# RWKV prep in a two-layer decoder trunk: weight splits of the k, r and v projections issued ahead, both pieces of a tile together

## The chip, the core and the metric

The kernel runs as one launch on one NeuronCore of a Trainium2 chip. The metric is the device time of one execution in microseconds (us); lower is better. Engines are named as in the profile: PE (TensorE matmul), DVE (VectorE), ACT (ScalarE), POOL (GpSimd), SP (SyncE, which here issues nearly all DMAs), and PEld for PE's weight loads.

## What is computed

Two layers, each on 512 tokens of width 1024 in float32. Of one layer:

```
h   = RMSNorm(x)
[q,k,v | r,k,v,lora_w,lora_a,lora_g | gate_A,gate_B] = h @ W_in
A   = sliding-window attention(q,k,v) -> W_oA
B   = RWKV-7 time mixing(r,k,v,decay,iclr,g) -> W_oB
x  += RMSNorm((sigmoid(gate_A)*A + sigmoid(gate_B)*B) @ W_out)
x  += RMSNorm(W_down(gelu(a)*b)),  [a,b] = causal conv3(RMSNorm(x) @ W_up)
x  += RMSNorm(sigmoid(x @ W_pg) * (p[i] @ W_ple))
```

The time mixing is a recurrence per head (16 heads of 64):

```
def step(state, inp):
    r_t, w_t, k_t, v_t, a_t, b_t = inp
    sa = einsum('bhvk,bhk->bhv', state, a_t)
    state = state * w_t[:,:,None,:] + sa[...,None] * b_t[:,:,None,:] + v_t[...,None] * k_t[:,:,None,:]
    return state, einsum('bhvk,bhk->bhv', state, r_t)
```

## The kernel before

Activations lie transposed, 128 channels by 512 tokens to a tile, eight tiles for h. Float32 products are made of three passes in a reduced type: weight and activation are each split into a high and a low part, and `mm3` (lines 247 to 252) issues high x high (L250), high x low (L251) and low x high (L252) into the same PSUM tile. A projection of one output tile has 8 such triples, 24 matmuls, and its weights come in two pieces of four row blocks (128 x 512 elements, 256 KB each). `load_w` (line 136) handles a piece in three steps: SP issues the DMA into `w`, ACT copies it into `wh` (L125), and DVE writes `wl = w - wh` (L155). Of the class "m" there are 2 buffers for `w`, 3 for `wh` and 3 for `wl` (line 141). `proj` (line 254) loads one piece, issues its 12 matmuls, loads the next piece, issues its 12; `whole` (line 208) loads both pieces before any matmul. Two PSUM tiles `pm` and one `pf` take the results.

The RWKV part of a layer works in four groups of two preps (`rwkv_group`, line 738). A prep (`rwkv_prep`, line 585) handles one channel tile, two heads: projection k, two small lora matmuls (`thw`, `tha`), a decay scan on DVE, the tile `AR`, projection r, small masked products `A` (PSUM, 2 buffers, written out by DVE as `AM`), transposes `bkT`, projection v, and transposes of v. In the text the preps of a layer are counted from 0 to 7, so prep 5 is the second of group 2 when groups are counted from 0 to 3. After two preps `rwkv_inverse` (line 672) inverts a triangular system: 31 steps of two short DVE operations each (L697, L699), a round trip through DRAM (`zd` out, eight DMAs `Z` back), and then, per prep of the group, a chain PE, ACT, PE, ACT/DVE of 32 x 32 products (t1 at L718, z12 at L727). Then eight scan steps over chunks of 64 tokens follow (L770 to L797), each a chain PE, DVE/ACT, PE, DVE/ACT, PE, DVE, and a group norm on DVE whose result is transposed on PE (`yt`, L822) and stored.

Beside this stand the gate projection (`w_gb`, matmuls on `pf` and `pm`) and, after it, the output projection of attention (`att_out`, `w_oa`, 8 tiles), whose 512-column matmuls can be put between the small ones; then the projection `w_or` reads what the four groups stored (`yr`).

No order is written out by hand. A scheduler orders each engine's instructions when the program is built: by its own estimates of times it takes the next instruction that could run, preferring the one that stands earlier in the program. `high_priority(offset=n)` lets the instructions of a block count as if they stood n places earlier. At run time each engine, SP's DMA queue included, works strictly in the order that was built.

Of the kernel before, what the change touches and what calls it, by code (L numbers as in the profile page):

```python
# [19 lines left out]
P = 128  # L20
T = 512
DM = 1024
KT = DM // P
# [32 lines left out]
class Trunk:  # L56
# [528 lines left out]
    def rwkv_prep(self, l, j, gi, R, X2, DC, ssp, nd):  # L585
        nc, a, h, vv, dv, rp = self.nc, self.a, self.h, self.vv, self.dv, R.rp
        NP_ = 32
        c1 = slice(j, j + 1)
        Tm = R.T
        q = Ctx()  # L590

        def ch(t):
            return t.rearrange("p (c t) -> p c t", t=C)
        k = self.shift(self.proj(a["w_k"][l, j], h), "k", j, Tm("k"))
        wa2 = self.load_w(a["w_wa2"][l, j], 2, low=((slice(64, 128), slice(0, 1)), (slice(0, 64), slice(1, 2))))
        th, ta = Tm("thw"), Tm("tha")
        for i, (t, n) in enumerate(((th, "w0h"), (ta, "a0h"))):
# [30 lines left out]
            self.tt(bk[:, :, x, :], ch(us[x]), ch(Di), ALU.mult)  # L628
        self.ts(ta, ta, dv["ka1"][:, c1], dv["ka2"][:, c1])
        self.tt(k, k, ta, ALU.mult)  # L630
        r = self.shift(self.proj(a["w_r"][l, j], h), "r", j, Tm("r"))
        self.tt(rv, ch(r), ch(D), ALU.mult)
        self.stt(r, r, vv("r_k")[:, c1], k, ALU.mult, ALU.mult)

# [15 lines left out]
        for hf in range(2):  # L650
# [4 lines left out]
            t = rp.tile([P, 4, P], F32, name="bkT", tag="bkT", bufs=6)  # L655
            self.act(t, tp.rearrange("p (c x) -> p c x", c=4))
            q.bkT.append(t)
        v = self.shift(self.proj(a["w_v"][l, j], h), "v", j, Tm("v"))
        bon = self.PT("bonus")
        self.last_prep = nc.tensor.matmul(bon, self.blockones, r, start=True, stop=True).ins  # L660
        vp = self.PT("vT")
# [540 lines left out]
```

## Time and profile before

| | us |
|---|---|
| median of 3 runs (lowest, highest) | 2319.58 (2317.64, 2322.39) |
| profiled execution, its own time | 2329.03 |
| span of the profiled execution | 2327.3 |

The profile is one execution. Its page gives PE busy for 96% of the span, PEld 75%, DVE 66%, ACT 48%. PE's granted clock (2.4 GHz at full speed, 1.2 GHz at half) is listed as a share of full speed; the mean over the span is 0.981. A busy PE is not PE at its peak: at half clock a matmul counts as busy twice as long. The two layers run the same program, so layer 0 (RWKV part about 200 to 640 us) and layer 1 (about 1350 to 1790 us) show the same stages twice.

### The profile page before, as it was taken

What the parts mean: (1) busy time and instruction counts of PE and PEld (TensorE: products, weight loads), DVE (VectorE), ACT (ScalarE), POOL (GpSimd) and SP (SyncE); (2) the same over time, 40 slices, a digit from 0 to 9 for tenths busy, and PEclk for the clock granted to TensorE, in tenths of its full rate; (3) what the DMA queues carried; (4) which work ended last, traced back from release to release, by engine and by line L of the source; (5) the groups of instructions that cost most, each with busy time, mean ns of one, the idle gap of its engine ahead of it and who ended that gap; (6) DMA issues with size and microseconds to landing.
All of it is one profiled execution on the core that took longest, in us unless ns stands there. A gap on an engine that the chain in (4) does not pass through costs nothing. (4 is left out here: it accounts for less than half of the span.)

```text
span 2327.3 us, 39473 instructions
## 1 busy us (share of the span) xinstructions
PE 2228.8 (96%) x14340; PEld 1740.2 (75%) x14340; DVE 1546.9 (66%) x3683; ACT 1109.6 (48%) x2450; POOL 27.1 (1%) x86
## 2 busy tenths in 40 slices
PE   7999999999999999999899999998999999999997
PEld 6766776667689777788896677766777887777886
DVE  6764678767566777743877647778656667776346
ACT  5566455544444544432445655545443544444332
POOL 1000000000000000000000000000000000000000
PEclk9999999889999999999999999999999999999998
DMA  4532332245571423233234333333356623223432
GB/s 150 168 94 97 99 94 79 75 121 171 176 259 31 128 91 98 89 118 116 86 124 148 98 104 98 83 92 103 113 159 212 213 78 92 95 95 90 126 98 69
DMA packets 204515, 269.40 MB, mean 116 GB/s; under 512 B 71840, under 2 KB 84640, under 8 KB 204320
## 3 DMA queue, kind: packets, MB, share of 16 engines
q1 hardware_dynamic: 204320, 266.88, 37.3%
q8 instruction: 113, 1.85, 0.3%
q14 instruction: 82, 0.67, 0.1%
HBM read 218.95 MB, written 42.47 MB: 112 GB/s over the span
## 5 line engine op out<-in xcount | busy, mean ns | idle before, releaser
L155 DVE TENSOR_TENSOR wl<-w,wh 128x512 fp32r<-128x512 f32 (+2 forms) x574 | 373.9, 662 | 317.4 <-ACT wh L125 292.7
L125 ACT ACTIVATE wh<-w 128x512 fp32r<-128x512 f32 (+1 forms) x590 | 348.8, 604 | 477.8 <-PE pm L251 134.7
L250 PE MATMUL pm<-hh,wh 128*128 128x512 f32 x1040 | 423.0, 412 | 4.6 <-ACT wh L125 2.4
L252 PE MATMUL pm<-hh,wl 128*128 128x512 f32 x1040 | 417.1, 408 | 7.4 <-DVE wl L155 7.2
L251 PE MATMUL pm<-hl,wh 128*128 128x512 f32 x1040 | 416.3, 404 | 0.0
L250 PEld LDWEIGHTS pm<-hh,wh 128*128 128x128 f32 x1040 | 196.8, 189 | 63.3 <-ACT wh L125 11.2
L252 PEld LDWEIGHTS pm<-hh,wl 128*128 128x128 f32 x1040 | 196.9, 189 | 57.5 <-DVE wl L155 13.6
L251 PEld LDWEIGHTS pm<-hl,wh 128*128 128x128 f32 x1040 | 197.4, 190 | 44.1 <-issue 7.2
L250 PE MATMUL pf<-hh,wh 128*128 128x512 f32 x512 | 208.3, 407 | 9.5 <-ACT hh L125 3.6
L251 PE MATMUL pf<-hl,wh 128*128 128x512 f32 x512 | 203.7, 398 | 0.0
L252 PE MATMUL pf<-hh,wl 128*128 128x512 f32 x512 | 203.5, 398 | 0.1
L134 DVE SCALAR_TENSOR_TENSOR cv<-un,vec,cv 128x511 f32<-128x511 f32 (+1 forms) x176 | 130.5, 749 | 40.6 <-ACT cv L125 38.1
L250 PEld LDWEIGHTS pf<-hh,wh 128*128 128x128 f32 x512 | 96.2, 188 | 42.7 <-ACT wh L125 8.5
L252 PEld LDWEIGHTS pf<-hh,wl 128*128 128x128 f32 x512 | 96.6, 189 | 27.0 <-issue 4.4
L251 PEld LDWEIGHTS pf<-hl,wh 128*128 128x128 f32 x512 | 96.7, 189 | 19.6 <-issue 1.8
L125 ACT ACTIVATE cv<-un,vec 128x512 f32<-128x512 f32 x88 | 71.1, 814 | 66.7 <-DVE un L128 66.7
L250 PE MATMUL pm<-uh,wh 128*128 128x512 f32 (+1 forms) x248 | 89.2, 360 | 3.5 <-ACT wh L125 3.4
L252 PE MATMUL pm<-uh,wl 128*128 128x512 f32 (+1 forms) x248 | 89.3, 360 | 0.0
L251 PE MATMUL pm<-ul,wh 128*128 128x512 f32 (+1 forms) x248 | 88.9, 359 | 0.0
L128 DVE TENSOR_TENSOR acc<-acc,sq 128x256 f32<-128x256 f32 (+1 forms) x114 | 50.0, 463 | 31.2 <-ACT sq L125 30.5
L533 DVE CUSTOM_DVE_ANT_0 sm<-scores,tmask 128x256 f32<-128x256 f32 (+1 forms) x128 | 43.5, 385 | 37.3 <-PE scores L117 37.1
L697 DVE TENSOR_TENSOR Z<-rin,Z 128x126 f32<-128x126 f32 (+22 forms) x248 | 62.3, 251 | 4.3
(409 smaller groups left out, 4468.9 us busy)
## 6 DMA issues: line engine op xcount, KB each, us to landing
w<-in_w_up_dram SPq DMA_DIRECT2D x156, 256.0 KB
w<-in_w_dn_dram SPq DMA_DIRECT2D x80, 256.0 KB
w<-in_w_q_dram SPq DMA_DIRECT2D x32, 256.0 KB
w<-in_w_ga_dram SPq DMA_DIRECT2D x32, 256.0 KB
w<-in_w_k_dram SPq DMA_DIRECT2D x32, 256.0 KB
w<-in_w_r_dram SPq DMA_DIRECT2D x32, 256.0 KB
w<-in_w_v_dram SPq DMA_DIRECT2D x32, 256.0 KB
w<-in_w_gb_dram SPq DMA_DIRECT2D x32, 256.0 KB
```

Source lines behind the costliest of these rows:

```text
L125: return self.nc.scalar.activation(out=out, in_=in_, func=func, **kw)
L128: return self.nc.vector.tensor_tensor(out=out, in0=in0, in1=in1, op=op)
L134: return self.nc.vector.scalar_tensor_tensor(out=out, in0=in0, scalar=s, in1=in1, op0=op0, op1=op1)
L155: self.nc.vector.tensor_tensor(out=wl, in0=w, in1=wh.bitcast(F32), op=ALU.subtract)
L250: mm(ps, wh, ah, start=start, stop=False)
L251: mm(ps, wh, al, start=False, stop=False)
L252: return mm(ps, wl, ah, start=False, stop=stop).ins
L533: nc.vector.tensor_tensor_reduce(out=sm[i][:, par * 256:par * 256 + KW], in0=scs[par][:, x * 256:x * 256 + KW], in1=tm, scale=1.0, scalar= ...
L697: nc.vector.tensor_tensor(out=tv, in0=rin[:, jj:jj + 1, jj + 1:].broadcast_to([P, n, nt]), in1=zt[:, :n, jj:jj + 1].broadcast_to([P, n, nt ...
```

## The change

In `rwkv_prep` the three calls of `proj` are replaced by `pr(ahead(name))`. `ahead` calls `whole`, so both pieces of a projection's weights are loaded and split before any of its matmuls, and it does so under `high_priority(offset=60)`: DMA, ACT copy and DVE subtraction of these pieces count as 60 places earlier in the program. `pr` then issues the same 24 matmuls into one PSUM tile. Nothing is added or left out: on every engine the same instructions stand, in another order.

```diff
-        k = self.shift(self.proj(a["w_k"][l, j], h), "k", j, Tm("k"))
+        def ahead(name):
+            with self.tc.high_priority(offset=60):
+                return self.whole(a[name][l, j], P, "m")
+
+        def pr(ws):
+            ps = self.PM("m")
+            for i, w in enumerate(ws):
+                self.mm3(ps, w, h[i], i == 0, i == KT - 1)
+            return ps
+        k = self.shift(pr(ahead("w_k")), "k", j, Tm("k"))
...
-        r = self.shift(self.proj(a["w_r"][l, j], h), "r", j, Tm("r"))
+        r = self.shift(pr(ahead("w_r")), "r", j, Tm("r"))
...
-        v = self.shift(self.proj(a["w_v"][l, j], h), "v", j, Tm("v"))
+        v = self.shift(pr(ahead("w_v")), "v", j, Tm("v"))
```

Three places show how the built order differs. The first is ACT in layer 0, prep 5, from its decay scan (`Di`, `DC`) to the inverse of group 1 (`t_3871` is t1's copy out of PSUM). Before:

```order
L125 ACTIVATE Di<-Di 128x512
L125 ACTIVATE DC<-D 128x8
L125 ACTIVATE kksq<-ss 128x512
L125 ACTIVATE thw<-tha,pq_580,pq_579 128x512
L125 ACTIVATE gt<-pf 128x512
L125 ACTIVATE u_4602<-tha,pq_582,pq_581 128x512
L125 ACTIVATE yo<-yt,vec 128x512
L125 ACTIVATE r<-pm,om_r 128x512
L125 ACTIVATE wh<-w 128x512 x2
L125 ACTIVATE t_3871<-t_3873 32x256
L125 ACTIVATE t_3871<-t_3874 32x256
L125 ACTIVATE Z<-z_3894 32x8x32
```

Now:

```order
L125 ACTIVATE wh<-w 128x512
L125 ACTIVATE D<-Di 128x512
L125 ACTIVATE kksq<-k,vec 128x512
L125 ACTIVATE Di<-Di 128x512
L125 ACTIVATE DC<-D 128x8
L125 ACTIVATE thw<-tha,pq_580,pq_579 128x512
L125 ACTIVATE kksq<-ss 128x512
L125 ACTIVATE u_4602<-tha,pq_582,pq_581 128x512
L125 ACTIVATE yo<-yt,vec 128x512
L125 ACTIVATE r<-pm,om_r 128x512
L125 ACTIVATE wh<-w 128x512
L125 ACTIVATE v<-pm,om_v 128x512
```

Before, both pieces of v's weights (`wh x2`) were copied after r had left PSUM; now one is copied ahead of the decay scan and the projection v is evacuated (`v<-pm`) before the inverse starts. On PE v's 24 matmuls thus stand ahead of and between prep 5's products `A`, where 3 of them stood before the inverse.

The second place is PE in layer 0, inverse of the last group (3), its second half (`z_5868`, `z_5869` are z12; L718 and L727 of before are L727 and L736 now), into the first scan steps. Before:

```order
L718 MATMUL t_5849<-zT,AM 32x32
L251 MATMUL pf<-hl,wh 128x512
L252 MATMUL pf<-hh,wl 128x512
L727 MATMUL z_5868<-Z,t_5846 32x32 x8
L250 MATMUL pf<-hh,wh 128x512
L727 MATMUL z_5869<-Z,t_5846 32x32 x8
L772 MATMUL xs<-X_5262,AM 64x64 x4
L251 MATMUL pf<-hl,wh 128x512
L252 MATMUL pf<-hh,wl 128x512
L778 MATMUL xs<-scr,Z 64x64 x4
L250 MATMUL pf<-hh,wh 128x512
L251 MATMUL pf<-hl,wh 128x512
```

Now:

```order
L727 MATMUL t_5849<-zT,AM 32x32
L736 MATMUL z_5868<-Z,t_5846 32x32 x8
L736 MATMUL z_5869<-Z,t_5846 32x32 x8
L781 MATMUL xs<-X_5262,AM 64x64 x4
L787 MATMUL xs<-scr,Z 64x64 x4
L794 MATMUL sp<-X_5262,bkT 64x64 x4
L797 MATMUL xs<-X_5262,AM 64x64 x4
L250 MATMUL pm<-hh,wh 128x512
L251 MATMUL pm<-hl,wh 128x512
L779 MATMUL xs<-ST_608,AR 64x64 x8
L781 MATMUL xs<-X_5262,AM 64x64 x4
L252 MATMUL pm<-hh,wl 128x512
```

The matmuls of `w_oa` that stood between the links of this chain now stand ahead of it.

The third place is SP's queue in layer 0 around the round trip of the same inverse (`mad` and `ta` are `att_out`'s store and load). Before:

```order
L122 DMA yrd_591<-yo 128x512
L122 DMA zd_3_5712<-Z 1024x1x32 x2
L122 DMA tbd_6225<-gt 128x512
L122 DMA o<-atd_1159 128x512
L122 DMA ta<-tad_2044 128x512
L122 DMA Z<-zd_3_5712 32x8x32 x8
```

Now:

```order
L122 DMA tbd_6225<-gt 128x512
L122 DMA zd_3_5712<-Z 1024x1x32 x2
L122 DMA yrd_591<-yo 128x512
L122 DMA mad_6578<-ta 128x512
L122 DMA ta<-tad_2044 128x512
L122 DMA Z<-zd_3_5712 32x8x32 x8
```

Between the two halves of the round trip a store of `yo` and a store of `ta` now stand, where a load of `o` and one of `ta` stood.

## Rows read from the trace of the kernel before

**Rows 1.** The page: busy time by engine.
```profile
PE 2228.8 (96%) x14340; PEld 1740.2 (75%) x14340; DVE 1546.9 (66%) x3683; ACT 1109.6 (48%) x2450; POOL 27.1 (1%) x86
```

**Rows 2.** Stretches: PE, PEld, DVE, ACT, POOL busy, then clock, DMA share, GB/s.
```profile
372.30:397.30 25.00, 20.75 (x112) 14.38 (x111) 24.07 (x65) 13.58 (x24) 1.22 (x4) 1.00 0.35 96
397.30:460.00 62.70, 61.94 (x640) 42.69 (x641) 41.50 (x114) 30.41 (x82) 0.53 (x1) 0.81 0.26 73
460.00:490.30 30.30, 26.10 (x128) 18.71 (x127) 24.98 (x65) 14.15 (x26) 1.22 (x4) 0.94 0.44 117
...
1527.30:1552.30 25.00, 20.74 (x112) 14.37 (x111) 24.07 (x65) 13.56 (x24) 1.22 (x4) 1.00 0.37 97
1552.30:1605.40 53.10, 51.23 (x628) 34.96 (x628) 39.98 (x109) 30.03 (x81) 0.53 (x1) 0.97 0.30 83
1605.40:1636.20 30.80, 26.29 (x160) 19.92 (x160) 27.17 (x70) 15.04 (x28) 1.22 (x4) 0.94 0.47 122
```

**Rows 3.** Timeline of PE: start, duration, line, form, [idle before <- releaser].
```profile
389.20 0.50 PE L252 MATMUL pm<-hh,wl 128*128 128x512 f32 x1 [1.37 <-DVE wl L155]
...
391.60 0.39 PE L250 MATMUL pm<-hh,wh 128*128 128x512 f32 x1
391.83 0.39 PE L251 MATMUL pm<-hl,wh 128*128 128x512 f32 x1
...
397.26 1.16 PE L117 MATMUL A<-AR,bk 64*128 64x128 f32 x16 [2.38 <-DVE AR L128]
398.83 0.79 PE L250 MATMUL pm<-hh,wh 128*128 128x512 f32 x1 [0.40 <-ACT wh L125]
```

**Rows 4.** Timeline of PE, the same place in layer 1.
```profile
1544.20 0.50 PE L252 MATMUL pm<-hh,wl 128*128 128x512 f32 x1 [1.37 <-DVE wl L155]
...
1552.26 2.08 PE L117 MATMUL A<-AR,bk 64*128 64x128 f32 x16 [2.38 <-DVE AR L128]
```

**Rows 5.** The view of stretches again: stretches at half clock, layers 0 and 1.
```profile
398.40:422.20 23.80, 23.40 (x227) 16.53 (x226) 6.67 (x15) 5.34 (x15) 0.00 (x0) 0.50 0.25 58
...
493.90:507.60 13.70, 13.70 (x152) 10.22 (x148) 6.16 (x15) 4.31 (x13) 0.00 (x0) 0.50 0.23 58
...
1552.00:1555.50 3.50, 3.24 (x19) 2.40 (x19) 1.99 (x4) 1.26 (x2) 0.00 (x0) 0.51 0.55 114
...
1644.20:1654.50 10.30, 10.30 (x88) 7.56 (x90) 4.28 (x11) 2.50 (x9) 0.00 (x0) 0.50 0.24 64
```

**Rows 6.** Timeline of PE, layer 0: prep 7's `A` and the inverse of group 2.
```profile
490.33 0.48 PE L117 MATMUL A<-AR,bk 64*128 64x128 f32 x2
490.75 0.69 PE L718 MATMUL t<-zT,AM 32*32 32x32 f32 x32
...
493.55 0.90 PE L117 MATMUL A<-AR,bk 64*128 64x128 f32 x8
```

**Rows 7.** Timeline of PE, layer 0: group norm's transpose, then the last inverse.
```profile
545.16 1.09 PE L822 MATMUL yt<-ident,Y 128*128 128x128 f32 x8 [0.17 <-DVE Y L128]
...
564.57 0.69 PE L718 MATMUL t<-zT,AM 32*32 32x32 f32 x32
565.19 0.50 PE L250 MATMUL pf<-hh,wh 128*128 128x512 f32 x1
...
565.85 0.69 PE L727 MATMUL z<-Z,t 32*32 32x32 f32 x16
...
574.29 0.50 PE L252 MATMUL pf<-hh,wl 128*128 128x512 f32 x1
```

**Rows 8.** Timeline of SP's queue at that inverse: start, time to issue, xcount.
```profile
554.73 1.29 SPq L122 DMA_DIRECT2D zd<-Z  x2
...
559.48 4.92 SPq L122 DMA_DIRECT2D Z<-zd  x8
```

**Rows 9.** Timeline of DVE at that inverse.
```profile
563.32 0.69 DVE L134 SCALAR_TENSOR_TENSOR ta<-ta,pm 128x512 f32<-128x512 f32 x1 [1.22 <-PE pm L252]
563.92 0.44 DVE L713 STREAM_TRANSPOSE zT<-Z 128x256 f32<-128x256 f32 x1
```

## The prediction

> **What bounds the kernel now.** I read the busy times first, then stretches of the RWKV part, then single waits in them. Over the whole span PE is the bound, busy 96% with DVE at 66% [rows 1], so what counts is time that PE loses: idle gaps, and work at half clock. The preps 5 to 7 of each layer are the exception. Between the products `A` of prep 4 and those of prep 5 (the first stretch of each layer in [rows 2]) PE is busy 20.75 of 25.00 us and DVE 24.07; in the stretch of preps 6 and 7 (the third) PE 26.10 of 30.30 and DVE 24.98, in layer 1 PE 26.29 and DVE 27.17 of 30.80. There DVE is the local bound and PE waits for it. The middle stretches belong to PE again: 61.94 of 62.70 and 51.23 of 53.10.
>
> The single waits of prep 5 are alike in both layers: 1.37 us for DVE's second split `wl` of projection r, 2.38 us ahead of `A` for DVE's tile `AR`, and in layer 0 another 0.40 for ACT's copy `wh` of v's weights [rows 3, 4]. While PE stands 2.38 us waiting for `AR`, no matmul of v can fill in, because v's weights come after `AR` in the order.
>
> The clock is the second loss. PE ran at 1.2 GHz, half of full, for 23.80 us right after that wait in layer 0, but for 3.50 us after the same wait in layer 1; and for 13.70 and 10.30 us in the inverse that follows prep 7 [rows 5]. The four make 51.3 us.
>
> **What the change does, part by part.** The sum is made against the profiled execution (2329.03, span 2327.3), which is 9.45 above the median of 2319.58. Every engine has the same instructions as before, so only waits and clock can change.
>
> (a) Prep 5's waits. v's two pieces are now copied ahead of the decay scan, and on PE all 24 of its matmuls are ready ahead of or between the `A`, where 3 stood before the inverse. At a pitch of 0.23 us (391.60 to 391.83 [rows 3]) some 19 matmuls more are 4.4 us of work, against 1.37 + 2.38 + 0.40 = 4.15 of waiting in layer 0 and 3.75 in layer 1. The work covers the waits if DVE reaches `AR` about when it did. DVE has 0.93 us to spare in this stretch (25.00 - 24.07) and gets at most two splits more ahead of `AR`, each near 0.60, the step of DVE from one 128x512 operation to the next [rows 9]: 1.2 against 0.93, so `AR` moves by a few tenths. I take the whole: -7.9 (bounds -7.9 and 0).
>
> First the row: both gaps ahead of `AR` are 2.38, both for `wl` are 1.37, with DVE named as releaser [rows 3, 4] and busy 24.07 of 25.00 [rows 2]. The Trainium skill ("Perfetto Trace Analysis", section "Identifying the Most-Contended Engine") says that one and the same bubble, repeated, can mean too few buffers for the next tile. By that rule a new order would leave the gaps, and the sum would be 7.9 higher; a DVE that is 96% busy was not standing for a buffer, so the trace speaks against it here.
>
> (b) Preps 6 and 7. They are bound by DVE. Their splits change places among DVE's work, none goes away, and PE's 4.2 us of waiting (30.30 - 26.10 [rows 2]) come back elsewhere. I take 0; the bounds per layer are -4.2 and +1.5 (two or three more splits of 0.60 ahead of `AR`).
>
> (c) Inverse of group 1, which now comes when v's matmuls of prep 5 have been used up. Its chain keeps about six large matmuls between the links where it had nine. Beside the last inverse such a filler takes 0.33 us (two of them fill 565.19 to 565.85 [rows 7]); three are 1.0, and with as many missing ahead of the chain I take +2.0 per layer, +4.0 in all (bounds 0 and +5).
>
> (d) The group norm of group 2. Its transposes `yt` wait 0.17 us for DVE's `Y` [rows 7]. With two more splits of 0.60 [rows 9] ahead of `Y` on DVE that is +1.2 per layer, +2.4 in all (bounds 0 and +3).
>
> (e) The last inverse of layer 0. Between 564.57 and 574.29 [rows 7] its links had 14 matmuls of `w_oa` between them; now they stand ahead and nothing hides the copies of ACT and DVE between the links. Fourteen at about 0.31 are 4.4 us (bounds 1.4, if the links themselves close up, and 4.7). Ahead of it, SP puts the eight `Z` loads behind a store of `ta`, and that tile needs the last matmul of a projection first: DVE waited 1.22 us for PE at just that addition [rows 9]. `Z` was issued 4.75 us after `zd` and took 4.92 us to issue [rows 8]. SP standing still there delays `t1` by half of one such issue, 2.4 (bounds 0 and 4). Together +6.8. Layer 1's last inverse keeps fillers: 0.
>
> The row gives 4.92 us of SP's time for eight loads [rows 8]. The Trainium skill ("DMA: Bandwidth & Descriptors", section "Issuing engines are not separate DMA queues") says that the time in which a sequencer initiates a DMA is usually small beside the DMA. By that rule a later place in SP's queue would cost next to nothing, and the sum would be 2.4 lower; the row, 0.6 us for each load, speaks for counting it.
>
> Without clock: -7.9 + 0 + 4.0 + 2.4 + 6.8 = **+5.3**. The waits alone make the kernel slower.
>
> (f) Clock. Price first: the middle stretch took 62.7 us in layer 0 and 53.1 in layer 1 [rows 2]. Of the difference of 9.6, 12 matmuls more are 2.7, and PE's idle time was 1.1 shorter (0.76 against 1.87), so 8.0 go with 20.3 us more at half clock (23.80 - 3.50 [rows 5]): 0.39 us for each. If prep 5's wait goes, I expect the two stretches after it to go: 27.3 x 0.39 = -10.6. The inverse after prep 7 lay at half clock where `A` of prep 7 is interleaved with `t1` and the other links, small products in a row [rows 6]. In the new order all of these `A` stand between v's matmuls and 12 large ones follow before `t1`: 24.0 x 0.39 = -9.4. New: the last inverse of layer 0 without fillers, as long as the stretch of 10.30: +4.0; the thinner inverse of group 1, 5 us at half clock in all: +2.0. Together **-14.0** (bounds -20 and +4).
>
> Total: 5.3 - 14.0 = -8.7. On the median, 2319.58 - 8.7 = 2310.9 if ordinary executions carry the same stretches. The 20.3 us more of layer 0 are worth 7.9 of the 9.45 by which the profiled execution exceeds the median, so they may be that execution's own, and then the median can win only 0.8 (2318.8). I give that a quarter: 2310.9 + 2.0 = **2313**.
>
> **The rivals.** *No change (2319).* DVE stays the bound of prep 5 as of preps 6 and 7: two splits more stand ahead of `AR`, and PE runs out of v's matmuls and waits there nevertheless. Then (a) is nothing and its stretches of half clock stay in part: 2310.9 + 7.9 = 2318.8. The long stretch being the profiled execution's own gives the same time. For it: DVE's 24.07 of 25.00. Against: PE gets 4.4 us of work for 4.15 us of waiting. The buffers of `wl` as the cause are part of this rival, at 0.05.
>
> *Slower (2329).* The inverse loses its cover, in layer 0's last group above all, and the clock gives nothing back: half clock moves from prep 7's place to the last inverse and to group 1's, and the stretches after prep 5 re-form as its small products still stand close together. Then it is 2319.58 + 5.3 + 4.0 = 2328.9. It decides from where half clock no longer falls by more than 5.3 - 4.6 = 0.7 us' worth, that is 2 us of the 51.3. For it: the terms without clock are all of known sign but one. Against: the large matmuls now stand beside all `A` of preps 5 and 7.
>
> That the change doesn't do what it says is excluded by the built order, in which the copies and v's matmuls have moved.
>
> **How the numbers follow.** This kernel's measurement can tell about 0.2%, 4.6 us, from no change: faster is below 2314.9, slower above 2324.2. I give the forecast 0.49, no change 0.30, slower 0.21. The forecast's own range is 2304 (preps 6 and 7 win 4.2 in one layer, and (c) or (d) falls to nothing) to 2315. The range of 8 in 10 leaves out a little below this and the upper part of the slower rival: 2304 to 2327.
>
> **What would show it.** (a): the waits ahead of prep 5's `A` are under 0.5 us in both layers while DVE stays over 90% busy; if they stay above 2 us, the first rival. (b): PE still idles about 4 us in the stretch of preps 6 and 7. (c), (e): gaps of 0.2 to 0.6 us between the links of these inverses, 4 us in sum in layer 0's last, and 2 to 3 us ahead of its `t1`. (f): the stretches after prep 5 and in the inverse after prep 7 run at 1.00; if the after-profile's half clock in these places and the new ones is still 45 us or more, I am wrong by the second rival.

## The result and the profile after

The changed kernel takes 2299.23 us (median of 4 runs, 2297.27 to 2304.48) against 2319.93 us of the kernel before (4 runs): a ratio of 0.991, 95% interval 0.9894 to 0.9926. That is 20.7 us faster, where 7 were forecast, and below the low end of the range, 2304. Its profiled execution took 2297.27 us, 31.8 less than that of before (2329.03). Of these, 11 come from which executions were profiled: that of before lay 9.1 above its median, this one 2.0 below its own.

The page of the changed kernel, its span, its busy times by engine and the clock in 40 slices, beside [rows 1]:

```profile
span 2295.5 us, 39457 instructions
PE 2207.6 (96%) x14340; PEld 1723.1 (75%) x14340; DVE 1542.2 (67%) x3683; ACT 1108.4 (48%) x2450; POOL 26.6 (1%) x86
PEclk9999999998999999999999999999999999999998
```

PE issues the same 14340 matmuls and is busy 21.2 us less. Work was not saved; a matmul at half clock counts twice as long (0.39 and 0.79 us for `pm` on L250 in [rows 3]), and fewer of them run there. The same stretches as in [rows 2], `A` of prep 4 to 5, 5 to 6 and 6 to 7, and after them the one long stretch at half clock that the RWKV part has left (PE, PEld, DVE, ACT, POOL busy, then clock, DMA share, GB/s):

```profile
371.70:396.70 25.00, 24.42 (x131) 17.93 (x130) 24.93 (x64) 13.68 (x25) 1.22 (x4) 1.00 0.41 105
396.70:446.10 49.40, 47.40 (x618) 31.72 (x617) 37.16 (x103) 29.14 (x79) 0.53 (x1) 1.00 0.33 93
446.10:474.20 28.10, 26.07 (x135) 19.19 (x134) 27.07 (x77) 15.33 (x28) 0.05 (x1) 1.00 0.38 114
550.70:567.80 17.10, 15.25 (x209) 11.41 (x207) 5.54 (x15) 6.57 (x21) 0.00 (x0) 0.50 0.40 132
...
1506.60:1531.60 25.00, 24.42 (x129) 17.91 (x128) 24.93 (x64) 13.60 (x25) 1.23 (x4) 1.00 0.41 107
1531.60:1580.90 49.30, 47.31 (x618) 31.75 (x617) 37.12 (x103) 29.14 (x79) 0.53 (x1) 1.00 0.33 93
1580.90:1608.40 27.50, 23.36 (x125) 16.96 (x124) 27.03 (x78) 14.73 (x27) 0.12 (x1) 1.00 0.39 116
```

Prep 4 to 5 still takes 25.00 us, but PE now does 131 matmuls there instead of 112. Layer 0's middle stretch falls from 62.7 to 49.4 us, with 22 matmuls fewer (618 against 640) and at full clock instead of 0.81.

The timeline of PE at `A` of prep 5 in layer 0 (start, duration, form, idle time before in brackets) and at the last inverse, beside [rows 3, 7]:

```profile
396.14 0.39 PE L250 MATMUL pm<-hh,wh 128*128 128x512 f32 x1
396.36 0.39 PE L251 MATMUL pm<-hl,wh 128*128 128x512 f32 x1
396.68 1.16 PE L117 MATMUL A<-AR,bk 64*128 64x128 f32 x16
...
535.06 1.07 PE L831 MATMUL yt<-ident,Y 128*128 128x128 f32 x8
...
549.41 0.69 PE L727 MATMUL t<-zT,AM 32*32 32x32 f32 x32 [1.66 <-DVE zT L722]
550.53 1.64 PE L736 MATMUL z<-Z,t 32*32 32x32 f32 x32 [0.43 <-ACT t L125]
552.59 1.06 PE L727 MATMUL t<-zT,AM 32*32 32x32 f32 x32 [0.42 <-DVE zT L722]
554.08 1.72 PE L736 MATMUL z<-Z,t 32*32 32x32 f32 x32 [0.43 <-ACT t L125]
555.73 0.69 PE L781 MATMUL xs<-X,AM 64*64 64x64 f32 x8
557.01 0.69 PE L787 MATMUL xs<-scr,Z 64*64 64x64 f32 x8 [0.58 <-ACT scr L125]
558.12 0.69 PE L794 MATMUL sp<-X,bkT 128*64 128x64 f32 x8 [0.42 <-DVE X L789]
```

The wait of 2.38 us ahead of `A` is gone. The last inverse stands bare as foreseen, with 3.9 us of gaps ahead of it, between its links and in the first scan step, and from 550.7 on it runs at half clock.

Summed over the whole trace, PE's idle time up to its last instruction fell from 89.7 to 79.1 us (-10.6) and the time at half clock from 89.2 to 38.2 us (-51.0). At 0.39 us for each us at half clock that is -19.9; the two make -30.5 of the 31.8 us.

### The profile page after: what moved, and what is told of

Read it like the earlier page. It is cut to its first block, busy times and chain, and to the rows that moved or that the text cites. A ratio compares the mean times of both kernels' runs of the same rounds, so it can differ in the third digit from the quotient of the medians.

```text
span 2295.5 us, 39457 instructions
## 1 busy us (share of the span) xinstructions
PE 2207.6 (96%) x14340; PEld 1723.1 (75%) x14340; DVE 1542.2 (67%) x3683; ACT 1108.4 (48%) x2450; POOL 26.6 (1%) x86
## 5 line engine op out<-in xcount | busy, mean ns | idle before, releaser
L250 PE MATMUL pm<-hh,wh 128*128 128x512 f32 x1040 | 422.7, 411 | 1.9 <-ACT wh L125 1.2
L250 PEld LDWEIGHTS pm<-hh,wh 128*128 128x128 f32 x1040 | 195.5, 188 | 61.8 <-ACT wh L125 8.7
L250 PE MATMUL pf<-hh,wh 128*128 128x512 f32 x512 | 207.7, 406 | 9.7 <-ACT hh L125 3.6
L250 PEld LDWEIGHTS pf<-hh,wh 128*128 128x128 f32 x512 | 96.0, 188 | 43.1 <-ACT wh L125 9.0
L250 PE MATMUL pm<-uh,wh 128*128 128x512 f32 (+1 forms) x248 | 89.2, 360 | 2.9 <-ACT wh L125 2.9
L252 PE MATMUL pm<-uh,wl 128*128 128x512 f32 (+1 forms) x248 | 89.2, 360 | 0.0
L128 DVE TENSOR_TENSOR acc<-acc,sq 128x256 f32<-128x256 f32 (+1 forms) x114 | 49.9, 462 | 31.1 <-ACT sq L125 30.5
L708 DVE TENSOR_TENSOR Z<-Z 128x126 f32<-128x126 f32 (+22 forms) x248 | 62.1, 250 | 3.7
```

What stands on the lines that cost most here:

```text
L128: return self.nc.vector.tensor_tensor(out=out, in0=in0, in1=in1, op=op)
L250: mm(ps, wh, ah, start=start, stop=False)
L252: return mm(ps, wl, ah, start=False, stop=stop).ins
L708: nc.vector.tensor_tensor(out=zt[:, :n, jj + 1:], in0=zt[:, :n, jj + 1:], in1=tv, op=ALU.add)
```

## Experiments

Three questions were left by the trace: which of the moved splits does it, whether half clock is caused by the waits or by the small products, and what the bare last inverse costs.

The built order narrows the first without any run. With `whole` alone and no priority, every engine's order is that of the kernel before. With the priority on one piece at a time, as `proj` loads them, it is that of the changed kernel, on every engine. That both pieces of a tile are loaded together is therefore no part of the effect; the priority is all of it. The priority on k alone moves only a few of PE's matmuls.

### Which projection, which prep

r alone (the call of k goes back to `proj` as that of v does; in v alone those of k and r do), v alone, and all three in prep 5 alone:

```diff
...
-        v = self.shift(pr(ahead("w_v")), "v", j, Tm("v"))
+        v = self.shift(self.proj(a["w_v"][l, j], h), "v", j, Tm("v"))
```
```diff
-            with self.tc.high_priority(offset=60):
+            with self.tc.high_priority(offset=60 if j == 5 else 0):
```

> Only projection r is loaded and split under the priority; k and v stay as before. In the built order this moves r's second piece and gate matmuls ahead of prep 5's A, takes prep 7's A out of the inverse of group 2, and leaves large matmuls between the links of layer 0's last inverse (there are none in the changed kernel). Theory (the order around A counts, whichever weights fill it): 2293 to 2302 us; the waits of 1.37 and 2.38 us at prep 5 and the half clock after them are gone, and so are the 17 us of half clock at the last inverse. Rival (as written in the prediction: it is v's matmuls, ready early, that fill prep 5's wait): the 2.38 us wait ahead of A stays and the time is 2312 to 2319 us.

> Only projection v is loaded and split under the priority; k and r stay as before. In the built order prep 5's A still follow 22 matmuls of r directly and stand close to t1. Theory (order around A): the 2.38 us wait and half clock after it stay, 2314 to 2321 us. Rival (v's early weights are the cause of the gain): 2297 to 2305 us.

> k, r and v under the priority in prep 5 of each layer alone; the other seven preps of a layer keep the old place. The built order is nearly that of r alone. Theory: one displaced split at prep 5 sets the order of all that follows, so nearly all of the gain is here: 2293 to 2302 us. Rival (preps 6 and 7 bring a good part on their own): 2306 to 2314 us.

Measured, against 23 runs of the kernel before on the same chip (2325.16): r alone 2296.68, ratio 0.9879 (0.9864 to 0.9895); v alone 2326.36, 1.0012 (0.9988 to 1.0035); prep 5 alone 2292.23, 0.9872 (0.9857 to 0.9887). r alone came as the theory had it, prep 5 alone 0.8 us below its range, and v alone, 5 us above its range, gains nothing. PE's timeline of v alone shows why: both waits of prep 5 stand as in [rows 3].

```profile
389.31 0.50 PE L252 MATMUL pm<-hh,wl 128*128 128x512 f32 x1 [1.37 <-DVE wl L155]
...
397.35 1.16 PE L117 MATMUL A<-AR,bk 64*128 64x128 f32 x16 [2.38 <-DVE AR L128]
```

So the step was narrowed to r in prep 5, two weight pieces per layer:

```diff
+            with self.tc.high_priority(offset=60 if j == 5 else 0):
...
-        r = self.shift(self.proj(a["w_r"][l, j], h), "r", j, Tm("r"))
+        r = self.shift(pr(ahead("w_r")), "r", j, Tm("r"))
```

> Only projection r of prep 5 of each layer, two weight tiles in the whole program, under the priority. Theory (one displaced split sets the order of all that follows): as fast as r alone or prep 5 alone, 0.986 to 0.989 of before. Rival (k and v of prep 5, or r of the other preps, carry a part): 0.990 to 0.995.

> The changed kernel itself, on the chip of the three others, so that ratios can be compared. Expected ratio to the kernel before 0.988 to 0.991 (0.991 in the first comparison, where the executions of before were faster by 5 us than on the chip of the first experiments).

Measured, against 18 runs of before on the same chip (2324.02): r of prep 5 alone 2293.73, ratio 0.9873 (0.985 to 0.9897); the changed kernel 2307.79, 0.9929 (0.9902 to 0.9955), less of a gain than the 0.988 to 0.991 expected; why is told below. One projection of one prep gives all of the gain, and more than the whole change does. In the built order even less is enough: with only DVE's subtractions of these two pieces under the priority, and their DMA and ACT copy at the old place, the order of every engine is that of this kernel; with only DMA and copy under it nothing of this happens.

DVE's timeline of before at prep 5 (`k<-pm` is projection k leaving PSUM, the scan is the decay scan, the two `wl` are the splits of r):

```profile
378.70 0.74 DVE L134 SCALAR_TENSOR_TENSOR k<-pm,vec,k 128x511 f32<-128x511 f32 x1
...
382.25 1.21 DVE L605 TENSOR_TENSOR_SCAN Di<-rs,thw 128x512 f32<-128x512 f32 x1
...
388.47 0.68 DVE L155 TENSOR_TENSOR wl<-w,wh 128x512 fp32r<-128x512 f32 x1
...
391.56 0.68 DVE L155 TENSOR_TENSOR wl<-w,wh 128x512 fp32r<-128x512 f32 x1
...
396.42 0.69 DVE L128 TENSOR_TENSOR AR<-r,D 128x512 f32<-128x512 f32 x1
```

and of the changed kernel, where the first two `wl` are r's and the third is v's first piece:

```profile
378.15 0.68 DVE L155 TENSOR_TENSOR wl<-w,wh 128x512 fp32r<-128x512 f32 x1
379.08 0.68 DVE L155 TENSOR_TENSOR wl<-w,wh 128x512 fp32r<-128x512 f32 x1
381.85 0.74 DVE L134 SCALAR_TENSOR_TENSOR k<-pm,vec,k 128x511 f32<-128x511 f32 x1
385.00 1.22 DVE L614 TENSOR_TENSOR_SCAN Di<-rs,thw 128x512 f32<-128x512 f32 x1
...
389.34 0.69 DVE L155 TENSOR_TENSOR wl<-w,wh 128x512 fp32r<-128x512 f32 x1
...
395.46 0.68 DVE L128 TENSOR_TENSOR AR<-r,D 128x512 f32<-128x512 f32 x1
```

Before, DVE split r's first piece 6 us behind the start of the scan, though that piece had long been in SBUF: PE used its `wh` at 377.75, 11 us earlier. After r's last matmul came `A`, and the 2.38 us were the way from there through ACT (`r`) and DVE (`r`, `AR`) back to PE, with nothing else in PE's order. With r's splits ahead of the scan, r leaves PSUM 3.4 us earlier, counted from `A` of prep 4 (ACT's copy of `r` starts at 391.00 instead of 394.92, `A` at 371.70 instead of 372.26), and the same way back is covered by the matmuls of v and of the gate, which now are due after r.

### What makes half clock

First, ten useless matmuls in the wait of prep 5, in the kernel before:

```diff
+        pv = self.PM("m")
+        if j == 5:
+            with self.tc.issue_after(self.last_mm):
+                for i in range(10):
+                    fill = nc.tensor.matmul(pv, h[1][0][:, 0:P], h[i % KT][0], start=True, stop=True).ins
...
+            with self.tc.issue_after(fill) if j == 5 else ExitStack():
...
```

> The kernel before with ten useless 128x512 matmuls between projection r and A of prep 5 in each layer (their results are overwritten): 2.3 us of added work in the 2.38 us wait. Theory (half clock follows that idle time): PE does not idle ahead of A, the stretches of half clock after it (23.8 and 3.5 us in the profile of before) go, and the time falls by 4 to 10 us to 2309 to 2316. Rival (half clock follows from small products standing close together, or the long stretch was that profile's own): 2318 to 2324 us, with the stretches still there.

Measured 2321.93, ratio 0.9983 (0.9968 to 0.9998) to before's 2325.16: 3.2 us less, just short of the 4 to 10 expected. As a plain time this lies in the rival's range, since before itself took 5.6 us more on this chip than the 2319.58 from which both ranges were reckoned; so the trace decides. In the built order the 20 matmuls are added and nothing else changes its place. The windows (prep 4 to 5, prep 5 to 6, then the inverse after prep 7 in layers 0 and 1):

```profile
372.70:397.70 25.00, 23.06 (x120) 16.24 (x120) 24.09 (x65) 13.57 (x24) 1.22 (x4) 1.00 0.36 95
397.70:451.10 53.40, 52.83 (x640) 36.33 (x640) 41.41 (x113) 30.37 (x82) 0.53 (x1) 1.00 0.31 85
...
482.08:495.73 13.65, 13.65 (x146) 10.17 (x146) 6.16 (x15) 4.43 (x13) 0.00 (x0) 0.50 0.20 58
...
1625.54:1646.02 20.48, 20.48 (x184) 15.12 (x184) 7.08 (x18) 4.64 (x14) 0.00 (x0) 0.50 0.16 43
```

The same 640 matmuls that took 62.7 us in [rows 2] take 53.4 behind the filled wait, at 1.00: 9.3 us for 23.8 us at half clock, 0.39 for each. Ten matmuls in each layer that compute nothing made the program faster. But in this execution the inverse after prep 7 lay at half clock for 13.65 and 20.48 us (13.70 and 10.30 in [rows 5]); the 10 us more in layer 1 eat part of the gain. There PE was busy all the time, and in the 12 us ahead of either stretch no wait stands.

The ten traces of this case, two layers each, agree on the wait of prep 5. Where it stands (the kernel before, v alone, and the filled inverse below) half clock followed between `A` of prep 5 and of prep 6 in all six cases, for 3.2 to 23.9 us. Where it is gone or filled, half clock came there in two of fourteen: 3.4 us in r alone and 20.5 us in the second profile of the changed kernel.

Second, useless matmuls in that inverse, again in the kernel before:

```diff
+    def fill(self, ps, after):
+        with self.tc.issue_after(after):
+            for i in range(KT):
+                x = self.nc.tensor.matmul(ps[:, 256:512], self.h[1][0][:, 0:P], self.h[i][0][:, 0:256], start=True, stop=True).ins
+        return x
...
+            f1 = self.fill(t1p[0], mm.ins) if grp == 2 else mm.ins
+            if grp == 2:
+                self.fill(z12[0], mm.ins)
```

> The kernel before with useless 128x256 matmuls, eight behind each t1 and each z12 of the inverse of group 2 in both layers (their results are never read): 32 per layer, 3.5 to 4.5 us of added work at full clock, next to prep 7's small products A. Theory (half clock there, 13.7 and 10.3 us in the profile of before, follows from small products without large ones between them, with no idle time ahead): the stretches vanish, which gives back 9 us, and the time is 0 to 4 us less than before. Rival (half clock follows from the idle time earlier, in preps 6 and 7): the stretches stay, and the time is 7 to 10 us more than before.

Measured 2318.53, ratio 0.9984 (0.9963 to 1.0006) to before's 2324.02: 5.5 us less, a little beyond the 0 to 4 of the theory, with an interval that still holds no change; the rival's 7 to 10 us more are outside it. The build also put some 160 of PE's other matmuls in other places, so the time is not that of the fillers alone. The windows of this inverse in the two layers:

```profile
485.60:505.60 20.00, 19.71 (x341) 15.16 (x344) 10.31 (x27) 8.36 (x26) 0.00 (x0) 1.00 0.26 75
1631.70:1651.70 20.00, 19.92 (x336) 15.68 (x336) 9.73 (x28) 8.36 (x28) 0.00 (x0) 1.00 0.23 63
```

At 1.00 throughout, with 64 matmuls more in the program. By their mean clocks the 12 runs spent 57 us at half clock on average, the 18 of before 85 (the filled wait: 75 against 87). Two situations brought half clock here: a wait of 2.4 us next to small products, and small products in a row without any wait. In both, larger matmuls put in between brought that place back to 1.00.

The price comes out of whole executions too. Over the 23 runs of before, whose mean clock went from 0.977 to 0.987 and whose time from 2334 to 2311, time rises by 0.42 us for each us at half clock ((1 - clock) x 2 x span); over the 12 of the filled kernel by 0.39, over the 18 of before on the other chip by 0.36.

### What the bare last inverse costs

The change in preps 0 to 5 only; layer 0's last inverse then keeps large matmuls between its links:

```diff
-            with self.tc.high_priority(offset=60):
+            with self.tc.high_priority(offset=60 if j < 6 else 0):
```

> The change in preps 0 to 5 of each layer; preps 6 and 7 stay as before. In the built order layer 0's last inverse then keeps large matmuls between its links, where the changed kernel has none, 3.9 us of idle PE and 17.1 us at half clock. Theory: those go, 5 to 9 us less than the changed kernel on the same chip. Rival (the large matmuls kept for the inverse are missing later, and half clock re-forms elsewhere): within 2 us of the changed kernel.

Measured 2296.02, ratio 0.9884 (0.9854 to 0.9913): 11.8 us less than the changed kernel's 2307.79 in the same comparison, more than the 5 to 9 expected, with intervals that overlap slightly. Its own trace has these 10 us of the last inverse at 1.00, with PE busy for 9.92. In r of prep 5 alone, which has the same order there, PE's timeline and the window show the chain covered:

```profile
555.76 0.69 PE L727 MATMUL t<-zT,AM 32*32 32x32 f32 x32
556.38 0.50 PE L252 MATMUL pm<-hh,wl 128*128 128x512 f32 x1
556.72 0.40 PE L250 MATMUL pm<-hh,wh 128*128 128x512 f32 x1
557.04 0.69 PE L736 MATMUL z<-Z,t 32*32 32x32 f32 x16
...
555.70:565.70 10.00, 10.00 (x166) 7.04 (x167) 2.57 (x6) 3.18 (x9) 0.00 (x0) 1.00 0.54 185
```

Part of the 11.8 is something else. The profiled execution of the changed kernel on this chip has, beside the last inverse, 20.48 us at half clock in layer 1's inverse of group 1, which its first profile doesn't have at all:

```profile
553.03:570.10 17.07, 15.22 (x209) 11.37 (x207) 5.54 (x15) 6.55 (x21) 0.00 (x0) 0.50 0.41 132
1546.31:1566.79 20.48, 19.96 (x198) 13.37 (x197) 5.47 (x16) 6.42 (x20) 0.00 (x0) 0.50 0.35 99
```

So the 11.8 us are not the price of the bare inverse alone, which stays an estimate. The same bears on the changed kernel's gain in the two comparisons (0.991 and 0.9929, with overlapping intervals): by their mean clocks its runs spent 41 us at half clock in the first and 57 in the second, and 16 x 0.39 = 6 of the 8.6 us between its two medians. The kernel with r of prep 5 alone spent 32 us at half clock on average over its 6 runs, from their mean clocks, against 57 of the changed kernel's 7; 25 x 0.39 = 10 of the 14 us between them. Its shorter idle time (76.4 us in its profile, 83.6 in that of the changed kernel) is more than enough for the remaining 4.

## Why the prediction was wrong in size

The direction, the bound and the clock were right. The step that failed is the sum of the waits without clock: +5.3 forecast, about -7 measured. Of the 12 us between, 5.3 lie in (e), 3.0 in (d), 2.3 in (c) and 1.7 in (b). By the prediction's own steps, with PE's idle time and half clock between the same instructions in the two first profiles (us; before, changed, r of prep 5 alone):

| from, to | idle L0 | half clock L0 | idle L1 | half clock L1 |
|---|---|---|---|---|
| `A` of prep 4 to 5 | 4.25, 0.58, 0.56 | 0 throughout | 4.26, 0.58, 0.58 | 0.2, 0, 0 |
| `A` of prep 5 to 6 | 0.76, 2.00, 2.17 | 23.9, 0, 0 | 1.89, 1.99, 2.19 | 3.2, 0, 0 |
| `A` of prep 6 to `t1` of group 2 | 4.20, 2.32, 1.68 | 3.4, 0, 0 | 4.49, 4.64, 5.01 | 3.4, 0, 0 |
| from there to `t1` of group 3 | 0.56, 1.97, 0.34 | 13.7, 0, 0 | 0.74, 0.41, 0.70 | 10.2, 0, 0 |

(a) Held in size: -7.9 forecast, 3.67 + 0.40 + 3.68 = 7.75 measured. It came out by luck, as its reason was wrong in what moved. The wait of 1.37 us was for the first split of r, not the second, and it is r's splits on DVE, not v's pieces, that open the place which v's and the gate's matmuls fill; v alone gains nothing. `AR` didn't move by some tenths to later, as reckoned, but came about 0.4 us earlier from the start of the stretch. Nor was DVE's load what PE waited for: DVE is busy for 24.93 of the 25.00 us now and the waits are gone. The 2.38 us were a way through three engines, with DVE itself waiting 0.37 us for ACT's `r` in it.

The rule of the Trainium skill that was weighed there ("Perfetto Trace Analysis", where it stands in the section "Optimization Strategy": a bubble that repeats can mean too few buffers) does not hold for this bubble: the 2.38 us went in both layers with a new order and the same buffers.

(b) Taken as 0: 4.20 to 2.32 in layer 0, 4.49 to 4.64 in layer 1, -1.7 together, inside its bounds.

(c) +4.0 was too much, and none of it came in the chain. From `A` of prep 5 to that of prep 6 the idle time rose from 0.36 us (prep 5's 0.40 taken out) to 2.00 in layer 0 and by 0.1 in layer 1: +1.7. But no wait of 0.15 us or more stands between the links of this inverse (401.62 to 408.49 in layer 0); the waits come later, the largest 0.61 us for a weight copy `wh` and 0.81 for `thw`. With one third of its fillers gone the chain is still covered.

(d) +2.4 did not come: `yt` at 535.06 has no wait, and in layer 1 it waits 0.22 us where it was 0.27. Large matmuls stood ahead of it, and DVE's `Y` was there in time. The rest of the stretch up to `t1` of group 3, without the 1.66 us counted in (e), has 0.6 less in the two layers.

(e) +6.8 was mis-sized most. 1.66 us ahead of `t1` and 2.3 in the chain did appear, 3.9 in place of 6.8. The 2.4 booked for SP's queue are not in it: from the issue of `zd` to `zT` it took 9.19 us before (554.73 to 563.92 in [rows 8, 9]) and takes 8.14 now.

```profile
540.68 1.46 SPq L122 DMA_DIRECT2D zd<-Z  x2
545.48 3.84 SPq L122 DMA_DIRECT2D Z<-zd  x8
548.82 0.45 DVE L722 STREAM_TRANSPOSE zT<-Z 128x256 f32<-128x256 f32 x1
```

The round trip did not become longer; PE had run out of matmuls to put beside it. But the matmuls of `w_oa` that left the chain are done earlier, so the projection behind waits less for the last `yr`: 2.17 + 1.75 us in layer 0 became 0.56 + 0.98. That gives back 2.4. A moved cover is paid at one end and earned at the other, and the prediction booked the cost alone.

So the sum without clock, forecast as +5.3, is about -7 in the RWKV part (-7.75 - 1.7 + 1.7 - 0.6 + 1.5) and -10.6 over the whole trace; most of the rest (2.7 us) lies between the RWKV parts of the two layers, and no run shows why.

(f) The clock term was right: -14.0 forecast, and in the RWKV part 58.0 us at half clock became 17.1, -40.9 x 0.39 = -16.0. The two stretches after prep 5 and the two after prep 7 went, the last inverse got its own (17.1 us, with 15 forecast for this and group 1). The price of 0.39 held (0.36 to 0.42 over whole executions).

The last step, a quarter for the long stretch being that profile's own, cost 2 us. The stretch itself was long: 23.9 us is the most of the six cases with the wait. But the runs of before on the other chips have a mean clock of 0.977 to 0.987, the profiled one 0.981, so ordinary executions carry as much half clock, some of it elsewhere. Without that step the forecast had been 2310.9; with the waits as measured, 2319.6 - 7 - 16 = 2297, and it was 2299.

The slower rival needed half clock to stay; it fell. In the no-change rival the waits at prep 5 would have stayed; they went.

## What to carry over

Where a scheduler orders the work, look for the one operation whose place sets the rest: here two DVE subtractions per layer, of weights long loaded, stood behind a scan, and moving only them did more than moving all splits. When a filler leaves a chain, book both ends, the gap that it opens and the later wait that it shortens. On PE count two losses apart, idle time and time at half clock, for the second was the larger here and is invisible in the busy share.

The best version measured is r of prep 5 alone: 2293.73 us, 0.9873 (0.985 to 0.9897) of the kernel before and below the changed kernel in the same comparison (2307.79).

## What was not expected of the hardware

Useless matmuls can pay: 20 more of 128x512 in two waits made the program 0.17% faster (interval 0.02 to 0.32%), because 640 matmuls behind them ran at 1.00 in place of 0.81. And a stretch at half clock is not a fixed property of the program: the inverse of group 1 in layer 1 of the changed kernel ran at full clock in one profile and at half for 20.48 us in another, with 1.99 and 1.61 us of idle time between the same instructions. What decides between the two stays open.
